# In a turn of the expert stage, work on finished sums is called ahead of the weight conversion

## The chip, the cores and the metric

The kernel runs on one core of a Trainium2 chip. The metric is the device time of one execution in microseconds (us), lower is better. TensorE does the matmuls, ScalarE and VectorE the elementwise work and the reading of PSUM, GpSimd (POOL) some small work, and SyncE (SP) starts the weight loads.

## The reference

It computes a decoder trunk of two layers on 256 tokens of width 1024 in float32. Only the last part matters here, the channel mixer of layer 1, a mixture of 8 experts of which each token takes 2:

```python
for e in range(N_EXPERTS):           # 8 experts, D_FF_EXPERT = 3584
    out = out + gates[:, e:e + 1] * _swiglu(t, w_gate[e], w_up[e], w_down[e])
# _swiglu(h, g, u, d) = (silu(h @ g) * (h @ u)) @ d
```

Ahead of it stand the mixers of both layers and a dense SwiGLU, and behind it a residual add and a final RMSNorm. The change touches none of these.

## The kernel before

**Precision.** A float32 product is made of fast float32r matmuls: each weight tile `raw` is split into a rounded part `wh` (ScalarE, line 190) and a remainder `wl` (VectorE, line 191). `Gran.conv` does this *conversion* of one tile, and also issues the tile's load on SP's queue if it isn't under way. Seven `raw` buffers hold loads, four `wh`/`wl` buffers hold converted tiles.

**Steps.** An expert's 3584 hidden columns are worked on in 4 chunks of 896. A *step* of TensorE uses one converted tile: four for the gate product (`g0` to `g3`, PSUM tile `pg`), four for the up product (`u0` to `u3`, `pu`), four for the down product of the expert before (`d0` to `d3`, `pd`, the last of half size). From expert 1 on a chunk runs in the order g0 g1 d0 g2 g3 d1 u0 u1 d2 u2 u3 d3. Expert 0 has eight steps a chunk, without the `d`; behind expert 7 stand its own down steps. An expert with at most 64 tokens is *few*: both halves of the split go through TensorE in one matmul, so a step has 8 matmuls in place of 12.

**Turns.** `emit` writes the order out by hand, one turn per step, and TensorE, ScalarE and VectorE keep the order in which they are called. Turn n called, before: the conversion of the tile of step n+3; the work in `mid[n]` (ScalarE and VectorE); the matmuls of step n; the folds; the TensorE work in `end[n]`. What stands in `mid` and `end`:

- `low`: ScalarE copies the lower half of a gate or up sum to `lo`, from which `fold_` adds it on TensorE (used for few).
- `post`: SiLU of the gate sum on ScalarE (line 1025), or the product with the up sum on VectorE (line 1027), both into `h`.
- `transposes`: `turn` turns `h` on TensorE into `pt` (line 971), `parts` splits that into `g2` for the down product, which runs four chunks later.
- `gather` for the next expert, in chunk 2: `select`, `rows_`, `parts`, `turn`, `copies`.
- `rows_of`: when the last down step of an expert has run, the two halves of its sum `yd` (both `pd` banks) are split into `h` by ScalarE (line 230) and VectorE (line 231). The next expert's first `d0` writes the same two banks and so waits for it.
- `scatter` (TensorE) and `residual_` (VectorE) put the result back on `x`.

`split` (lines 229 to 231) is the helper of `rows_of` and of both `parts`, and tells them apart only by the tile names.

Of the kernel before, what the change touches and what calls it, by code (L numbers as in the profile page):

```python
# [46 lines left out]
def trunk_kernel(ctx: ExitStack, tc, x_in, attn_norm, ffn_norm, w_in, b_in, conv_w, conv_b,  # L47
# [809 lines left out]
    def expert_steps(rnd):  # L857
# [8 lines left out]
        order, mid, end, folds, whose = [], {}, {}, {}, {}  # L866

        def at(where, n, f):
            where.setdefault(n, []).append(f)

        def put(e, run, gran):
            whose[len(order)] = e
            order.append((gran, run))

        def last():
            return len(order) - 1

        def emit():
            for n in range(max([len(order)] + [i + 1 for i in (*mid, *end, *folds)])):
                for g, _ in order[n:n + AHEAD_E + 1]:  # L880
                    g.conv()
                for f in mid.get(n, ()):
                    f()

                mine = [f for e, f in folds.get(n, ()) if whose.get(n) == e]
                if n < len(order):
                    g, run = order[n]
                    run(g.h, g.l, mine)
                for e, f in folds.get(n, ()):
                    if f not in mine:  # L890
                        by_count(e, lambda few, f=f: few and f())
                for f in end.get(n, ()):
                    f()
# [86 lines left out]
        def proj(e, c, nm, w, pool):  # L980

            wv = w[0, e, :, c * CH:(c + 1) * CH].rearrange("(k p) f -> p k f", p=P)
            st = {}

            def step(k2):
                def run(wh, wl, extra):
                    if k2 == 0:
                        st["p"] = [moe[pool].tile([P, 512], F32, name=pool) for _ in range(2)]

                    def mms(few):  # L990
                        for kk in range(2):
                            k = k2 * 2 + kk
                            x_ = xg[e][:, k]
                            both = x_.rearrange("p h s -> p (h s)")[:, 0:2 * P:2]
                            for hc in range(2):
                                o = slice(hc * HC, (hc + 1) * HC)
                                products(st["p"][hc][:, :HC], (x_[:, 0, :], x_[:, 1, :], both), wh[:, kk, o],
                                         wl[:, kk, o], k == 0, k == KD - 1, few)
                        for f in extra * few:
                            f()  # L1000
                    by_count(e, mms)
                put(e, run, Gran((rnd, e, c, nm, k2), (2, CH), lambda t: [(t, wv[:, k2 * 2:k2 * 2 + 2, :])],
                              lambda t: t, DVE))
                if k2 == KD // 2 - 1:
                    if rnd == 0:
                        at(mid, last() + 1, low)
                        at(folds, last() + 3, (e, fold_))
                    at(mid, last() + 4, post)

            def low():  # L1010
                for hc in range(2):
                    nc.scalar.activation(moe["lo"][HP:, hc * HC:(hc + 1) * HC], st["p"][hc][HP:, :HC], AF.Copy)  # L1012

            def fold_():
                for hc in range(2):
                    nc.tensor.matmul(st["p"][hc][:HP, :HC], fold, moe["lo"][:, hc * HC:(hc + 1) * HC],
                                     start=False, stop=True, skip_group_check=True)

            def post():
                if nm == "g":  # L1020
                    gg[e, c] = tmp.tile([P, CH], F32, name="h", bufs=3)
                for hc in range(2):
                    ps, o = st["p"][hc][:, :HC], slice(hc * HC, (hc + 1) * HC)
                    if nm == "g":
                        nc.scalar.activation(gg[e, c][:, o], ps, AF.Silu, scale=rxs[e])  # L1025
                    else:
                        nc.vector.scalar_tensor_tensor(gg[e, c][:, o], ps, rxs[e], gg[e, c][:, o],  # L1027
                                                       op0=ALU.mult, op1=ALU.mult)
            return [lambda k2=k2: step(k2) for k2 in range(KD // 2)]

        yd, ys, pys = {}, {}, {}

        def down(e, c):
            wv = moe_w_down[0, e, c * CH:(c + 1) * CH, :].rearrange("(j p) c -> p j c", p=P)
            both = (0, 1)
            parts = [(0, both), (2, both), (4, both), (6, both)]
            if (e, c) == (NE - 1, NCH - 1):

                parts[2:] = [(4, (0,)), (6, (0,)), (4, (1,)), (6, (1,))]

            def step(j0, chs):
                j1 = min(j0 + 2, KJ)

                def run(wh, wl, extra):
                    if c == 0 and j0 == 0:
                        for ch in chs:
                            yd[e, ch] = moe["pd"].tile([P, 512], F32, name="pd")

                    def mms(few):
                        for j in range(j0, j1):  # L1050
                            g_ = gt[e, c][:, j]
                            b = g_.rearrange("p s h -> p (s h)")[:, :P]
                            for i, ch in enumerate(chs):
                                o = slice(i * 512, (i + 1) * 512)
                                products(yd[e, ch], (g_[:, :, 0], g_[:, :, 1], b), wh[:, j - j0, o], wl[:, j - j0, o],
                                         c == 0 and j == 0, c == NCH - 1 and j == KJ - 1, few)
                        for f in extra * few:
                            f()
                    by_count(e, mms)
                put(e, run, Gran((rnd, e, c, "d", j0), (j1 - j0, D), lambda t: [(t, wv[:, j0:j1, :])],  # L1060
                              lambda t: t[:, :, chs[0] * 512:(chs[-1] + 1) * 512], DVE))
                if c == NCH - 1 and j1 == KJ:
                    n = last()
                    if e < NE - 1:
                        at(mid, n + 1, lambda: rows_of(e, both))
                        for ch in both:
                            at(end, n + 10 + 3 * ch, lambda ch=ch: scatter(e, ch))
                            at(mid, n + 11 + 3 * ch, lambda ch=ch: residual_(e, ch))
                    else:
                        at(mid, n + 1, lambda: rows_of(e, chs))  # L1070
                        at(end, n + 1, lambda: scatter(e, chs[0]))
                        at(mid, n + 2, lambda: residual_(e, chs[0]))
            return [lambda a=a: step(*a) for a in parts]
# [13 lines left out]
        def residual_(e, ch):  # L1087
            for t in range(NT):
                xs = x[:, t, ch * 512:(ch + 1) * 512]
                nc.vector.scalar_tensor_tensor(xs, pys[t], moe["gates"][:, t, e:e + 1], xs,  # L1090
                                               op0=ALU.mult, op1=ALU.add)
# [7 lines left out]
        for e in range(NE):  # L1099
            for c in range(NCH):  # L1100
                g = proj(e, c, "g", moe_w_gate, "pg")
                u = proj(e, c, "u", moe_w_up, "pu")
                d = down(e - 1, c) if e > 0 else []
                n0 = len(order)
                for fs, n in ((g, 2), (d, 1), (g, 2), (d, 1), (u, 2), (d, 1), (u, 2)):
                    do(fs, n)
                turn, parts = transposes(e, c)
                at(end, last() + 6, turn)
                at(mid, last() + 7, parts)
                do(d, 1)  # L1110
                if c == 2 and e + 1 < NE:
                    for (w, n), f in zip(((mid, 6), (end, 9), (mid, 10), (end, 12), (mid, 13)), gather(e + 1)):
                        at(w, n0 + n, f)
        for c in range(NCH):
            d = down(NE - 1, c)
# [2 lines left out]
        def run():  # L1118
            select, rows_, parts, turn, copies = gather(0)
            select()  # L1120
            for q in range(2):
                rows_((q,))
            parts()
            if rnd == 0:
                moe["flags"]()
                moe["weights"]()
            turn()
            copies()
            E = mybir.EngineType
            with tc.manual_schedule(engines={E.PE, E.Activation, E.DVE}):  # L1130
                emit()
# [58 lines left out]
```

## Time and profile before

| | |
|---|---|
| median of 3 runs | 1425.63 us (1423.59 to 1430.9) |
| the profiled execution's own time | 1431.23 us |
| its span, first to last instruction | 1429.5 us |
| its mean granted TensorE clock | 0.959 |

The profile shows one execution. Times in a timeline count from the start of the span. An engine's idle time is put down to the instruction that came last by the profile; where several are waited for, the name may be that of another.

### The profile page before, as it was taken

The page shows a single profiled execution, that of the slowest core. Times are in us where ns is not written, and L with a number is a line of the kernel's source. Part 1 is how long each engine was busy: PE and PEld are TensorE (multiplying, and loading weights), DVE is VectorE, ACT ScalarE, POOL GpSimd, SP SyncE. Part 2 cuts the span into 40 slices and gives each one's busy share as a digit, 9 for nine tenths or more (in the row PEclk, how much of TensorE's full clock was granted, in tenths as well). Part 3 has the DMA queues.
Part 4 walks back from the last instruction along what each step waited for, and adds up shares of the span by engine and source line. Part 5 has one row for each costly group of instructions (what it writes and reads, how often), then busy time and mean ns, then how long its engine had stood idle before and what let it go on. Part 6 is the DMA issues. An engine that isn't in the chain of part 4 may idle for free.

```text
span 1429.5 us, 18911 instructions
## 1 busy us (share of the span) xinstructions
PE 1315.3 (92%) x6899; PEld 1141.3 (80%) x6899; DVE 1164.2 (81%) x1155; ACT 1020.8 (71%) x1120; POOL 143.3 (10%) x98
## 2 busy tenths in 40 slices
PE   6989999989996879899999999899999899999986
PEld 6857999979765767687888889788888788888865
DVE  7785555567757878999999887899998999989975
ACT  5646444445745868898888777788887888878863
POOL 5551111117431000000000000000000000000000
PEclk9899999999898989999999999999999999999998
DMA  8823555663223998999999998899999999999991
GB/s 247 231 90 120 193 189 181 198 169 119 83 67 125 373 332 303 406 404 401 372 392 357 345 361 324 318 388 398 367 361 405 363 353 393 377 372 374 406 346 48
DMA packets 150176, 416.21 MB, mean 291 GB/s; under 512 B 8598, under 2 KB 49634, under 8 KB 150048
## 3 DMA queue, kind: packets, MB, share of 16 engines
q1 hardware_dynamic: 149760, 413.38, 79.6%
q8 instruction: 89, 1.46, 0.4%
q0 software_dynamic: 288, 1.05, 0.2%
q14 instruction: 39, 0.32, 0.1%
HBM read 413.35 MB, written 1.05 MB: 290 GB/s over the span
## 4 chain that ended last, share of the span: by engine, by line
PE 70%; DVE 11%; ACT 8%; issue 7%; DMA 2%; POOL 1%; SPq 0%; DVEq 0%; ACTq 0%; POOLq 0%
PE pu L909 17%; PE pd L909 16%; PE pg L909 9%; ACT wh L190 5%; DVE wl L191 5%; PE mm L693 4%; PE acc L718 4%; PE mm L351 4%; PE cv L693 4%; DVE cv L428 2%; PE pt L934 2%; PE acc L576 2%; PE pt L971 2%; PE acc L493 1%; DMA raw<-in_w_in_dram 1%
## 5 line engine op out<-in xcount | busy, mean ns | idle before, releaser
L191 DVE TENSOR_TENSOR wl<-raw,wh 128x1792 fp32r<-128x1792 f32 (+2 forms) x460 | 849.6, 1885 | 167.4 <-ACT wh L190 166.2
L190 ACT ACTIVATE wh<-raw 128x1792 fp32r<-128x1792 f32 (+2 forms) x496 | 755.9, 1555 | 302.5 <-PE pd L909 80.1
L909 PE MATMUL pd<-wh,g 128*128 128x512 f32 x672 | 246.2, 408 | 23.2 <-ACT wh L190 17.1
L909 PE MATMUL pu<-wh,xg 128*128 128x448 f32 x768 | 251.8, 374 | 9.9 <-DVE h L1027 9.9
L909 PE MATMUL pg<-wh,xg 128*128 128x448 f32 x768 | 250.6, 372 | 5.2 <-ACT h L1025 5.2
L909 PE MATMUL pu<-wl,xg 128*128 128x448 f32 x512 | 192.1, 375 | 2.8 <-DVE wl L191 2.8
L909 PE MATMUL pg<-wl,xg 128*128 128x448 f32 x512 | 191.1, 373 | 1.8 <-DVE wl L191 1.6
L909 PE MATMUL pd<-wl,g 128*128 128x512 f32 x448 | 181.4, 405 | 0.9 <-DVE wl L191 0.9
L909 PEld LDWEIGHTS pd<-wh,g 128*128 128x128 f32 x672 | 132.6, 197 | 51.9 <-ACT wh L190 19.3
L909 PEld LDWEIGHTS pu<-wh,xg 128*128 128x128 f32 x768 | 148.7, 194 | 24.4 <-ACT lo L1012 11.0
L909 PEld LDWEIGHTS pg<-wh,xg 128*128 128x128 f32 x768 | 148.3, 193 | 20.4 <-ACT h L1025 7.5
L909 PEld LDWEIGHTS pg<-wl,xg 128*128 128x128 f32 x512 | 99.5, 194 | 15.2 <-DVE wl L191 7.0
L909 PEld LDWEIGHTS pu<-wl,xg 128*128 128x128 f32 x512 | 100.8, 197 | 13.6 <-DVE wl L191 5.1
L909 PEld LDWEIGHTS pd<-wl,g 128*128 128x128 f32 x448 | 88.1, 197 | 18.3 <-DVE wl L191 2.9
L428 DVE SCALAR_TENSOR_TENSOR cv<-up,wcol,cv 128x256 f32<-128x256 f32 x226 | 98.3, 485 | 5.1 <-PE cv L402 3.1
L1147 POOL DMA_DIRECT2D h<-in_final_norm_dram x1 | 0.6, 599 | 964.2 <-PE pt L1085 964.2
L191 POOL TENSOR_TENSOR wl<-raw,wh 128x1024 fp32r<-128x1024 f32 x36 | 86.1, 2406 | 38.9 <-ACT wh L190 38.7
L351 PE MATMUL mm<-th,wh 128*128 128x256 f32 x224 | 65.9, 297 | 1.1 <-ACT sg L409 1.1
L351 PE MATMUL mm<-tl,wh 128*128 128x256 f32 x224 | 65.5, 293 | 0.8 <-DVE tl L288 0.8
L351 PE MATMUL mm<-th,wl 128*128 128x256 f32 x224 | 65.4, 293 | 0.9 <-POOL wl L191 0.7
L718 PE MATMUL acc<-wh,pp 128*128 128x512 f32 x176 | 50.3, 396 | 0.0
L693 PE MATMUL cv<-tl,wh 128*128 128x256 f32 x176 | 49.3, 280 | 0.3 <-DVE tl L288 0.3
(232 smaller groups left out, 1711.4 us busy)
## 6 DMA issues: line engine op xcount, KB each, us to landing
raw<-in_moe_w_gate_dram SPq DMA_DIRECT2D x128, 896.0 KB
raw<-in_moe_w_up_dram SPq DMA_DIRECT2D x128, 896.0 KB
raw<-in_moe_w_down_dram SPq DMA_DIRECT2D x96, 1024.0 KB
raw<-in_moe_w_down_dram SPq DMA_DIRECT2D x32, 512.0 KB
raw<-in_ffn_w_gate_dram SPq DMA_DIRECT2D x11, 1024.0 KB
raw<-in_ffn_w_up_dram SPq DMA_DIRECT2D x11, 1024.0 KB
raw<-in_ffn_w_down_dram SPq DMA_DIRECT2D x11, 1024.0 KB
raw<-in_w_in_dram SPq DMA_DIRECT2D x10, 1024.0 KB
```

What stands on the lines that cost most here:

```text
L190: nc.scalar.activation(self.h, src, AF.Copy)
L191: (lo or lo_eng()).tensor_sub(self.l, src, f32(self.h))
L351: nc.tensor.matmul(ps[:, :S], w(a, k), b[:, k, :], start=(n == 0), stop=(n == 3 * KD - 1))
L428: nc.vector.scalar_tensor_tensor(acc, up[:, c, k:k + S], w, acc, op0=ALU.mult, op1=ALU.add)
L493: nc.tensor.matmul(o, qT[hp, j, n * P:(n + 1) * P], kT[hp, k0:(n + 1) * P], start=False, stop=True)
L576: nc.tensor.matmul(st["o"][t][c], a[:, k, tk], b[:, 0, c * 512:(c + 1) * 512], start=(first and i == 0), stop=(last and i == 2))
L693: nc.tensor.matmul(ps, a[:, k, :], b[:, k, :], start=(n_ == 0), stop=(n_ == 3 * KD - 1))
L718: nc.tensor.matmul(st["o"][t][cc], a[:, kk, tk], b[:, 0, cc * 512:(cc + 1) * 512], start=(first and i == 0), stop=(last and i == 2))
L909: nc.tensor.matmul(ps, a, b, start=(first and i == 0), stop=(last and i == len(mm) - 1))
L934: nc.tensor.matmul(ps[:, j, :], moe["hn"][:, t, d], st["Sm"][:, t, :], start=(t == 0), stop=(t == NT - 1))
L971: nc.tensor.transpose(ps[:, j - j0, :], g[:, j * P:(j + 1) * P], ident)
L1147: nc.gpsimd.dma_start(fg, final_norm.unsqueeze(0).to_broadcast([P, D]))
```

## The change

In `emit` the `mid` work is called ahead of the conversion instead of behind it. Of the entries in `mid`, `low`, `post`, `residual_` and two of `gather` are put one turn later. `parts` of the transposes goes two turns later and `turn`, its TensorE half in `end`, one. `rows_of`, `select`, and the `residual_` behind the very last steps keep their turn.

```diff
             for n in range(max([len(order)] + [i + 1 for i in (*mid, *end, *folds)])):
+                for f in mid.get(n, ()):
+                    f()
                 for g, _ in order[n:n + AHEAD_E + 1]:
                     g.conv()
-                for f in mid.get(n, ()):
-                    f()
...
-                        at(mid, last() + 1, low)
+                        at(mid, last() + 2, low)
                         at(folds, last() + 3, (e, fold_))
-                    at(mid, last() + 4, post)
+                    at(mid, last() + 5, post)
...
                         at(mid, n + 1, lambda: rows_of(e, both))
                         for ch in both:
                             at(end, n + 10 + 3 * ch, lambda ch=ch: scatter(e, ch))
-                            at(mid, n + 11 + 3 * ch, lambda ch=ch: residual_(e, ch))
+                            at(mid, n + 12 + 3 * ch, lambda ch=ch: residual_(e, ch))
...
-                at(end, last() + 6, turn)
-                at(mid, last() + 7, parts)
+                at(end, last() + 7, turn)
+                at(mid, last() + 9, parts)
                 do(d, 1)
                 if c == 2 and e + 1 < NE:
-                    for (w, n), f in zip(((mid, 6), (end, 9), (mid, 10), (end, 12), (mid, 13)), gather(e + 1)):
+                    for (w, n), f in zip(((mid, 6), (end, 9), (mid, 11), (end, 12), (mid, 14)), gather(e + 1)):
```

## Rows read from the trace of the kernel before

**Rows 1.** The page: engines' busy time, and the chain that ended last.
```profile
PE 1315.3 (92%) x6899; PEld 1141.3 (80%) x6899; DVE 1164.2 (81%) x1155; ACT 1020.8 (71%) x1120; POOL 143.3 (10%) x98
...
PE 70%; DVE 11%; ACT 8%; issue 7%; DMA 2%; POOL 1%; SPq 0%; DVEq 0%; ACTq 0%; POOLq 0%
```

**Rows 2.** Two stretches: length, busy us by engine, PEclk, DMA share, GB/s.
```profile
550.00:975.00 425.00, 403.29 (x1940) 349.91 (x1939) 387.07 (x264) 352.76 (x307) 0.00 (x0) 0.99 0.98 369
975.00:1365.00 390.00, 374.97 (x1817) 328.71 (x1815) 360.75 (x248) 326.06 (x285) 0.00 (x0) 0.99 1.00 379
```

**Rows 3.** Waits, 550 to 1365: us in total, times, longest.
```profile
DVE wl L191 <- ACT wh L190: 66.3, 68, 4.4
ACT wh L190 <- PE pd L909: 60.7, 42, 3.3
...
PE pd L909 <- ACT wh L190: 17.1, 6, 4.2
...
PE pt L971 <- DVE h L1027: 13.5, 13, 1.8
```

**Rows 4.** Groups by form, 550 to 1365: busy us, mean ns, idle before.
```profile
L191 DVE TENSOR_TENSOR wl<-raw,wh 128x1792 fp32r<-128x1792 f32 x220 | 437.1, 2021 | 31.2 <-ACT wh L190 30.5
...
L1027 DVE SCALAR_TENSOR_TENSOR h<-pu,rx,h 128x448 f32<-128x448 f32 x56 | 35.6, 678 | 0.0
L191 DVE TENSOR_TENSOR wl<-raw,wh 128x1024 fp32r<-128x1024 f32 x28 | 34.2, 1222 | 0.0
...
L231 DVE TENSOR_TENSOR h<-pd,h 128x512 fp32r<-128x512 f32 x12 | 7.7, 683 | 0.0
```

**Rows 5.** ScalarE's timeline, end of an expert: start, length, idle before.
```profile
897.17 1.92 ACT L190 ACTIVATE wh<-raw 128x2048 fp32r<-128x2048 f32 x1 [2.15 <-PE pd L909]
899.12 0.97 ACT L1012 ACTIVATE lo<-pu 64x448 fp32r<-64x448 f32 x2
900.12 1.70 ACT L190 ACTIVATE wh<-raw 128x1792 fp32r<-128x1792 f32 x1
901.84 1.09 ACT L230 ACTIVATE h<-pd 128x512 fp32r<-128x512 f32 x2
```

**Rows 6.** VectorE's timeline at the same place.
```profile
899.13 2.29 DVE L191 TENSOR_TENSOR wl<-raw,wh 128x2048 fp32r<-128x2048 f32 x1 [2.04 <-ACT wh L190]
901.85 2.03 DVE L191 TENSOR_TENSOR wl<-raw,wh 128x1792 fp32r<-128x1792 f32 x1 [0.43 <-ACT wh L190]
903.79 1.28 DVE L231 TENSOR_TENSOR h<-pd,h 128x512 fp32r<-128x512 f32 x2
...
913.39 3.96 DVE L191 TENSOR_TENSOR wl<-raw,wh 128x1792 fp32r<-128x1792 f32 x2 [2.99 <-ACT wh L190]
```

**Rows 7.** TensorE's timelines: the first matmul into `pd` of each expert's sum.
```profile
656.49 0.47 PE L909 MATMUL pd<-wh,g 128*128 128x512 f32 x1 [1.67 <-ACT wh L190]
...
774.24 0.48 PE L909 MATMUL pd<-wh,g 128*128 128x512 f32 x1 [2.57 <-ACT wh L190]
...
904.62 0.77 PE L909 MATMUL pd<-wh,g 128*128 128x512 f32 x1 [4.25 <-ACT wh L190]
...
1021.31 0.47 PE L909 MATMUL pd<-wh,g 128*128 128x512 f32 x1 [2.16 <-ACT wh L190]
...
1140.99 0.48 PE L909 MATMUL pd<-wh,g 128*128 128x512 f32 x1 [4.24 <-ACT wh L190]
...
1256.93 0.47 PE L909 MATMUL pd<-wh,g 128*128 128x512 f32 x1 [2.17 <-ACT wh L190]
...
1371.02 0.76 PE L909 MATMUL pd<-wh,g 128*128 128x512 f32 x1 [6.15 <-DVE h L231]
```

**Rows 8.** TensorE's timeline: transposes in an expert with few tokens.
```profile
941.70 1.25 PE L971 MATMUL pt<-ident,h 128*128 128x128 f32 x7 [1.79 <-DVE h L1027]
```

**Rows 9.** Short stretches at two of those stalls, columns as in rows 2.
```profile
900.00:910.00 10.00, 5.75 (x15) 4.36 (x15) 9.57 (x8) 6.27 (x6) 0.00 (x0) 0.66 0.96 344
910.00:925.00 15.00, 15.00 (x75) 13.57 (x75) 12.01 (x9) 13.27 (x13) 0.00 (x0) 1.00 0.76 258
1015.00:1030.00 15.00, 12.84 (x56) 10.83 (x55) 11.80 (x10) 10.42 (x10) 0.00 (x0) 0.89 1.03 408
```

## The prediction

> **What bounds the kernel now.** I read the page first, then the waits, then timelines at the places that the waits name. The page has TensorE busy for 92% and on 70% of the chain that ended last, VectorE on 11% [rows 1]. That is a mean over stages; the change lies in the expert stage alone, so the stage comes next, cut at 550 and 1365 us (experts 1 to 7). There TensorE is busy for 403.29 + 374.97 = 778 of 815 us, VectorE for 387.07 + 360.75 = 748, ScalarE for 679, GpSimd for nothing, and the DMA share is 0.98 to 1.00 [rows 2]. Three resources lie within 8% of each other: what one of them gains is worth something only where the other two have room.
>
> TensorE's missing 37 us are what is to be had. The waits name two places [rows 3]: 17.1 us in 6 waits ahead of a matmul into `pd`, and 13.5 us in 13 waits of the transposes for `post`. The third large wait, ScalarE's conversion for TensorE (60.7 us), is that of an engine held back by a full set of `wh` buffers, and only follows TensorE.
>
> The timelines show the 6 waits, and a seventh at 1371.02, as one pattern: 1.67, 2.57, 4.25, 2.16, 4.24, 2.17 and 6.15 us, once per expert, always before the first down step `d0` of a new sum [rows 7]. Six are put down to ScalarE's conversion, the seventh to VectorE's `h`. I take the seventh to be right for all. At 904.62 the conversion of `d0`'s own tile (the one of 2048) had ended on ScalarE at 897.17 + 1.92 = 899.09, and on VectorE at 899.13 + 2.29 = 901.42, 3.2 us earlier [rows 5, 6]. What ended last is `rows_of`: VectorE began it at 903.79, and at 0.683 us a half [rows 4] its first bank was free at 904.47.
>
> **The change part by part.** First, what does not move. A turn was "conversion n+3, then mid n" and becomes "mid n, then conversion n+3". An entry that goes from mid n to mid n+1 at the same time is called between the conversions n+3 and n+4 in both versions. This holds for `low`, `post`, `residual_` and the gather's `parts` and `copies`: ScalarE and VectorE get the same instructions in the same order, in both kernels. No sum is read later than it was, and nothing waits less. The entries behind the last steps have no conversion left to pass. All of it: 0 us. SP's queue holds the loads alone, in the order of the conversions, so that isn't touched; GpSimd has no work in the stage [rows 2].
>
> What moves on its engine is what was not shifted by exactly one.
>
> (a) `rows_of` keeps turn n+1 and so passes one conversion, that of `g2` behind `d0`. Before, ScalarE's order was: conversion `d0` (897.17), `low` (899.12), conversion `g2` (900.12), `rows_of` (901.84) [rows 5], and VectorE's `d0`, `g2` (901.85), `rows_of` (903.79) [rows 6]. After: ScalarE is through with `low` at 900.09 and does its two copies by 901.2; VectorE ends `d0` at 901.42 and frees the first bank at 901.42 + 0.68 = 902.10, the second at 902.8. 904.47 becomes 902.10: 2.4 us earlier. It adds no wait, since the conversion of `d0` ahead of it has already waited for the same down step (2.15 us behind `pd`, at 897.17 [rows 5]). Behind it the conversion of `g2` comes 1.1 us later on ScalarE and about 1.3 us on VectorE, and TensorE wants it next.
>
> At the first six places the stall shrinks by up to 2.4 us: 1.67 + 2.4 + 2.4 + 2.16 + 2.4 + 2.17 = 13.2. At the seventh the tile passed is a half one, 1.222 us on VectorE [rows 4]: 1.2. Together 14.4. Then what is late next: `g2`. VectorE ends the two halves at 902.8 and `g2`'s remainder 2.02 us later, 904.8, which is 902.10 + 2.7. A down step of 12 matmuls takes longer than that, and one of 8 about 2 us, so at the three places where the finished down product is that of an expert with few tokens (656.49, 1021.31, 1256.93) some 0.4 us comes back: 13.2 in all, to the nearest.
>
> The clock is a second term. At the stall of 1021.31 the granted clock is 0.89 over 15 us, so 0.11 x 15 = 1.65 us of full-speed time goes with it; around 904.62 it is 0.66 over 10 us [rows 9], part of that while TensorE is idle anyway. Of the two levels, 1.2 and 2.4 GHz, it fell to the lower behind the idle time. The stalls at 1021.31 and 1256.93 should vanish, and with them 2 x 1.65 = 3.3 us. Those at 904.62 and 1140.99 keep 1.8 us and the last keeps 5, so I count nothing there. Bounds for the clock: 0, if the remaining gaps trip it as before, and 5 x 1.65 = 8.3. I take 3.3, because the two stalls that disappear are the ones that the row prices.
>
> Is there room on VectorE and in the loads for 13.2 + 3.3 = 16.5 us? Behind the stall of 904.62 VectorE stood for 2.99 us (913.39) and before it for 0.43 [rows 6], since ScalarE ran out of free buffers behind the stalled TensorE: there the stall is passed on whole, and about 3 us is what that place can give. And the DMA share fell to 0.76, 258 GB/s, in 910 to 925, for the same reason [rows 9]. So both have idle time at just these places, and it goes with the stall.
>
> (b) `turn`, the seven transposes, goes one TensorE step later, and `parts` one conversion later; `g2` is needed four chunks on, so nothing waits for it. Before, TensorE stood up to 1.79 us for `post` [rows 8], 13.5 us in 13 waits [rows 3]. After, it runs `d1` first, whose conversion stands ahead of `post` on VectorE and so is done, and `post` (two at 0.678 us [rows 4]) ends meanwhile. But these waits lie in experts with few tokens, where a TensorE step is shorter than a conversion's 2.02 us on VectorE [rows 4]: what TensorE saves it mostly waits later for `wl`. Bounds: 0 and 13.5. I take 2, nearer to 0, since VectorE is busy for 748 of 815 us [rows 2].
>
> (c) `select`, three VectorE instructions on 128 columns each, passes one conversion, as `parts` of (b) moves the other way by one. Each is shorter than the 0.678 us of `post` on 448 columns: under 2 us in 7 places, in a stretch in which the tile then late has the room that `parts` left. 0, bounds -1 and +2.
>
> Sum: 13.2 + 3.3 + 2 = 18.5 us. From the profiled execution's own 1431.23 that makes 1412.7; that execution lies 5.6 us above the median of the runs, so on runs like those it is 1425.63 - 18.5 = 1407, and I say 1408.
>
> **The rivals.** *The loads bind.* The DMA share is near 1 already [rows 2]; if the queue cannot go faster, what TensorE saves at a stall is waited for at a later load. For it: share 0.98 to 1.00. Against: the mean is (425 x 369 + 390 x 379) / 815 = 374 GB/s, while 408 is reached in a short stretch [rows 9], so at 408 the stage's bytes take 815 x 374 / 408 = 747 us, 68 us less. Room on average, though not in every chunk. If a third of the 18.5 arrives: 1420. The Trainium skill's page "DMA: Bandwidth & Descriptors" (section "Where 436 GB/s comes from") would have it bind: for transfers from HBM it gives about 358 GB/s for a core. By that rule this stage would be at its limit now and the change worth nothing, 1426. The rows, with 369 and 379 over hundreds of us and 408 in a stretch, are above the rule, for a core that runs alone; I go by them.
>
> *The change does nothing.* Most of its lines leave the order as it was, as shown; if the order of `rows_of` does not set the stall either, it is 1425.6. Against it: the seventh row names `rows_of`.
>
> *Slower: the profile's name is right, and `d0` does wait on ScalarE's conversion.* Six of seven rows say so [rows 7]. Then `rows_of`, put ahead of the conversion of `g2`, delays it by its own 1.28 us on VectorE [rows 6], seven times: 9 us, 1435. It decides if the stalls before `d0` stay as long as they were with `rows_of` done early. Against it: the tile's conversion was over 3.2 us before.
>
> *More than that.* The clock gives its whole 8.3 and the transposes half of their 13.5: 13.2 + 8.3 + 6.8 = 28, 1397.
>
> **How the numbers follow.** The forecast, 1402 to 1414, gets 0.68; more than that 0.10; the loads 0.10; nothing 0.06; slower 0.06. The range goes from 1398 to 1420: it takes in the forecast, nearly all of the larger gain and the case of the loads, and leaves out some 0.15. A change under 0.5%, about 7 us, is what a measurement of this kernel can't tell from none. Faster by more: the forecast, the larger gain, and a few hundredths of the loads, 0.82. Within 0.5%: the loads' rest and nothing, 0.12. Slower: 0.06.
>
> **What would show it.** In the profile of the changed kernel, ScalarE's `h<-pd` should stand right behind `lo<-pu` and ahead of the 1792-wide conversion; the idle time before the first `pd` matmul should be 0 at about four places, some 1.8 at two and 5 at the last; the granted clock should stay at 1.00 around the places that were 1021 and 1257. The wait of `pt` for `h L1027` should be gone, and small waits of `pu` or `pd` for `wl` should have grown. The order of all else on ScalarE and VectorE should be as before. The prediction is wrong if `d0` stalls as long as ever, if waits for `raw` appear on ScalarE, or if a conversion that found its buffer free before now waits for TensorE a step longer.

## The result, and the profile after

The changed kernel takes 1393.28 us, the median of 6 runs (1385.47 to 1395.55), against 1423.32 us for the kernel before beside it (6 runs, 1418.65 to 1430.9). The ratio is 0.977, with a 95% interval of 0.9741 to 0.98: about 33 us, or 28 to 37, where 18.5 were predicted. The direction was right; the time lies below the range. The profiled execution took 1386.59 us.

The page of the changed kernel, beside [rows 1]:

```profile
PE 1295.2 (94%) x6899; PEld 1124.6 (81%) x6899; DVE 1162.6 (84%) x1155; ACT 1019.3 (74%) x1120; POOL 143.3 (10%) x98
```

The work is the same (the counts of instructions are those of before), but TensorE is busy for 20 us less. Two profiled executions differ also in front of the expert stage, where the code is the same, so from here on the stage is cut from the first matmul into `pg` to the last scatter matmul. The windows of the whole stage, first of the kernel before and then of the changed one (columns: stretch, length, busy us of PE, PEld, DVE, ACT and POOL, granted clock, DMA share, GB/s):

```profile
453.34:1417.88 964.54, 905.74 (x4325) 787.91 (x4323) 861.18 (x593) 783.30 (x689) 0.60 (x1) 0.98 0.95 357
```

```profile
440.74:1373.40 932.66, 897.26 (x4325) 779.81 (x4323) 859.17 (x593) 782.00 (x689) 0.60 (x1) 0.99 0.96 369
```

The stage is 31.9 us shorter. TensorE's busy time fell by 8.5 us and its idle time by 23.4. The stretches that answer to [rows 2], and the one that answers to the second of [rows 9]:

```profile
530.00:955.00 425.00, 413.20 (x2000) 357.05 (x2001) 398.09 (x275) 364.71 (x319) 0.00 (x0) 1.00 1.00 378
955.00:1345.00 390.00, 382.33 (x1866) 335.24 (x1865) 371.91 (x253) 335.66 (x292) 0.00 (x0) 0.99 1.01 394
1000.00:1015.00 15.00, 15.00 (x76) 13.31 (x75) 15.00 (x11) 12.47 (x12) 0.00 (x0) 1.00 1.03 407
```

In as many us TensorE does more instructions than before, and behind the place that was 1021 (now 999.62) the granted clock stays at 1.00, where it was 0.89. The waits in 530 to 1345, beside [rows 3] (us in total, times, longest):

```profile
DVE wl L191 <- ACT wh L190: 44.2, 50, 5.7
ACT wh L190 <- PE pd L909: 38.0, 31, 5.3
...
PE pu L909 <- DVE wl L191: 4.6, 10, 1.1
PE pd L909 <- ACT wh L190: 4.1, 1, 4.1
PE pd L909 <- DVE wl L191: 3.6, 9, 1.0
```

The wait of the transposes (L971) for `h` is gone. Of the waits before the first matmul into `pd` one long one is left, the last. The wait that the prediction set aside, ScalarE's conversion for the down matmuls, fell as well, from 60.7 us [rows 3] to 38.0. The timelines of ScalarE and of VectorE at the place of [rows 5, 6], and TensorE's at five of the seven places of [rows 7]:

```profile
877.51 1.93 ACT L190 ACTIVATE wh<-raw 128x2048 fp32r<-128x2048 f32 x1 [0.76 <-PE pu L909]
879.46 0.98 ACT L1012 ACTIVATE lo<-pu 64x448 fp32r<-64x448 f32 x2
880.46 1.09 ACT L230 ACTIVATE h<-pd 128x512 fp32r<-128x512 f32 x2
881.43 3.31 ACT L190 ACTIVATE wh<-raw 128x1792 fp32r<-128x1792 f32 x2
```

```profile
879.47 2.29 DVE L191 TENSOR_TENSOR wl<-raw,wh 128x2048 fp32r<-128x2048 f32 x1 [0.66 <-ACT wh L190]
881.68 1.28 DVE L231 TENSOR_TENSOR h<-pd,h 128x512 fp32r<-128x512 f32 x2
883.17 6.16 DVE L191 TENSOR_TENSOR wl<-raw,wh 128x1792 fp32r<-128x1792 f32 x3 [0.21 <-ACT wh L190]
```

```profile
641.32 0.39 PE L909 MATMUL pd<-wh,g 128*128 128x512 f32 x1
...
756.03 0.48 PE L909 MATMUL pd<-wh,g 128*128 128x512 f32 x1 [0.70 <-PEq L899]
...
882.78 0.48 PE L909 MATMUL pd<-wh,g 128*128 128x512 f32 x1 [0.67 <-DVE h L231]
...
1106.39 0.48 PE L909 MATMUL pd<-wh,g 128*128 128x512 f32 x1 [0.86 <-DVE h L231]
...
1325.67 0.76 PE L909 MATMUL pd<-wh,g 128*128 128x512 f32 x1 [4.10 <-ACT wh L190]
```

`rows_of` stands where the prediction put it, and the stalls are 0.70, 0.67, 0.86 and 4.10 us and none at the three others. But look at the first line of ScalarE. In [rows 5] the conversion of `d0` began after 2.15 us of waiting, for a matmul into `pd`; here it waited 0.76 us, for one into `pu`. Nothing in the diff touches that conversion. It wants a free buffer, and it now wants another one.

The addresses in the two built programs say which. Most of the stage's 386 conversions write the buffers of the conversion four turns back, as a ring of four would. In the kernel before 34 take those of the conversion *three* turns back: 27 conversions of `d0` (every chunk from expert 1 on but the first), 6 of a `u0`, and one of expert 7's own down steps. The one behind each of them takes those of five turns back. I call the 34 *early*: an early one cannot start before TensorE is a step further on. The changed kernel has 8 such places.

### The profile page after: what moved, and what is told of

It is laid out like the page before. It is cut to its first block, busy times and chain, and to the rows that moved or that the text cites. A ratio compares the mean times of both kernels' runs of the same rounds, so it can differ in the third digit from the quotient of the medians.

```text
span 1384.9 us, 18931 instructions
## 1 busy us (share of the span) xinstructions
PE 1295.2 (94%) x6899; PEld 1124.6 (81%) x6899; DVE 1162.6 (84%) x1155; ACT 1019.3 (74%) x1120; POOL 143.3 (10%) x98
## 5 line engine op out<-in xcount | busy, mean ns | idle before, releaser
L909 PE MATMUL pd<-wh,g 128*128 128x512 f32 x672 | 239.3, 397 | 6.3 <-ACT wh L190 4.1
```

The lines of the kernel that those rows point to most:

```text
L909: nc.tensor.matmul(ps, a, b, start=(first and i == 0), stop=(last and i == len(mm) - 1))
```

## The experiments

Theory 1: the 31.9 us are the sum of `rows_of`, the transposes, and the choice of buffers. Theory 2, the rival: order alone made the gain, and the buffers are a by-product that costs nothing. All timed against the kernel before; "us" is (1 - ratio) x 1423; by the intervals one such number is good to 3 to 6 us, and a difference of two to some 5 to 9. The last two columns are from one profiled execution each, which is not always near the median: that of e3 took 1406.63 us, 9 above its median, most of it ahead of the stage, which began at 452.80 us there and at 444.23 in e1.

| kernel | early places | median us | ratio (95%) | us | stage us | TensorE busy |
|---|---|---|---|---|---|---|
| before | 34 | 1423 | 1 | | 964.5 | 905.7 |
| control, named buffers (e9) | 34 | 1426.18 | 1.0024 (0.9996 to 1.0052) | -3.4 | 965.7 | 906.5 |
| + `rows_of` (e11) | 34 | 1411.33 | 0.9928 (0.9899 to 0.9957) | 10.2 | 949.5 | 902.2 |
| + transposes (e12) | 34 | 1413.20 | 0.9942 (0.9918 to 0.9966) | 8.3 | 953.5 | 902.6 |
| changed order (e10) | 34 | 1400.02 | 0.9846 (0.9812 to 0.988) | 21.9 | 939.3 | 899.5 |
| before's order, in turn (e1) | 0 | 1401.18 | 0.9849 (0.9806 to 0.9892) | 21.5 | 939.9 | 893.7 |
| + `rows_of` (e2) | 0 | 1391.99 | 0.9772 (0.9735 to 0.9809) | 32.4 | 932.7 | 894.2 |
| + transposes (e3) | 0 | 1397.54 | 0.9807 (0.9772 to 0.9843) | 27.5 | 940.5 | 898.7 |
| changed order, in turn (e4) | 0 | 1387.48 | 0.9732 (0.9687 to 0.9777) | 38.1 | 929.0 | 895.2 |
| `rows_of`, pool's choice (e7) | 28 | 1411.16 | 0.9924 (0.9902 to 0.9946) | 10.8 | 950.3 | 901.5 |
| transposes, pool's choice (e8) | 14 | 1401.12 | 0.9845 (0.982 to 0.9871) | 22.1 | 943.6 | 899.8 |
| the changed kernel | 8 | 1393.28 | 0.977 (0.9741 to 0.98) | 32.7 | 932.7 | 897.3 |

**Buffers in turn (e1).** `Ring` hands out eight named tiles, four `wh` and four `wl`, in strict turn. Every engine has the same instructions in the same order as in the kernel before.

```diff
-        hl[0] = ctx.enter_context(tc.tile_pool(name="hle", bufs=AHEAD_E + 1, reuse_waits="tile"))
+        hl[0] = Ring(ctx.enter_context(tc.tile_pool(name="hle", bufs=1, reuse_waits="tile")), AHEAD_E + 1)
...
+    def tile(self, sh, dt, name):
+        free = self.free[name]
+        i = free.pop(1 if self.k[name] in self.early else 0)
+        self.k[name] += 1
+        free.append(i)
...
```

> The kernel before, with its order of work untouched: the four pairs of buffers for converted weights are taken strictly in turn in the expert stage, where before takes, at 34 of 386 conversions, the buffer freed last (that of the conversion three turns back instead of four). Theory 1 (the missed part of the gain is the choice of buffers): 34 conversions wait one step less, 26 of them not early any more in the changed kernel; by the shift of 0.3 to 0.5 us a place seen in the chunks without rows_of, 8 to 14 us faster than before, about 1412 us, and ScalarE's wait for the down product falls from 60.7 us to under 35. Theory 2 (the rows_of and the transposes make the whole gain, buffers are a by-product): within 3 us of before, about 1423.

Measured: 21.5 us (15 to 28) with no instruction moved, more than I expected.

**`rows_of` alone, and the transposes alone, over buffers in turn (e2, e3), and the changed order over them (e4).** In e2 a list `pre` is called ahead of the conversion and holds `rows_of` alone; e3 shifts two turns. e4 is the changed kernel with `Ring`.

```diff
+                for f in pre.get(n, ()): f()
                 for g, _ in order[n:n + AHEAD_E + 1]:
...
-                        at(mid, n + 1, lambda: rows_of(e, both))
+                        at(pre, n + 1, lambda: rows_of(e, both))
```

```diff
-                at(end, last() + 6, turn)
-                at(mid, last() + 7, parts)
+                at(end, last() + 7, turn)
+                at(mid, last() + 8, parts)
```

> The same kernel with buffers in turn, and in addition rows_of alone taken past one conversion (it stands ahead of it); transposes and parts stay. Theory 1: 12 to 16 us below the run with buffers in turn alone, about 1398; the wait of the first down product of each expert, 1.7 to 6.2 us in the kernel before, falls under 1 us. Theory 2: 18 to 25 us below that run. A third theory, that the transposes hold the most: at most 5 us below it.

> The kernel before with buffers in turn, and in addition the transposes alone one step later and the copies behind them one conversion later; rows_of stays where it was. Theory 1: 2 to 5 us below the run with buffers in turn alone, about 1408. Theory 2: 5 to 10 us below it. Third theory (the transposes hold the most): 15 us or more below it.

> The changed kernel with buffers in turn: only its 8 remaining early places go. Theory 1: 0 to 4 us below the changed kernel, about 1391, and equal within 3 us to before less the gains of the three runs beside it added up. Theory 2: as the changed kernel, 1393.

Measured against e1, by the ratios: `rows_of` 11.0 us, the transposes 6.0, and both with the rest of the change 16.6. So they add up, and 38.1 is 21.5 + 11.0 + 6.0 to within a us. In the profiled stages `rows_of` is worth 7.2 us and the transposes nothing (-0.6); that the transposes bring anything over buffers in turn is not shown, since the intervals of e1 and e3 overlap by much. (Those of e1 and e2 just touch, but every run of e2 is below every run of e1.) e4 is the fastest kernel here. It lies 5.4 us below the changed kernel by the ratios and 3.7 in the stage, but the intervals overlap.

**The early choice written out (e5, e6).** The named buffers, taken early at the 34 places, with the conversion still called ahead of the matmuls that read the buffer it takes.

```diff
+        hl[0] = Ring(ctx.enter_context(tc.tile_pool(name="hle", bufs=1, reuse_waits="tile")), AHEAD_E + 1, EARLY)
```

> A control for the four runs with buffers in turn: the kernel before with the same eight named buffers, but taken as before takes them, the one freed last at the same 34 places. Theory 1 (it is the choice that counts): as before, 1423 within 4 us. Theory 2 (naming the buffers changes something else, the waits that the builder places for instance, and that made the 21.5 us): about 1401, as the run with buffers in turn.

> The changed kernel, its order of work untouched, with the named buffers taken at the 34 places of the kernel before. Theory 1: only rows_of (9.2 us by the run before) and the transposes (3.6 us) remain of the gain, so about 13 us faster than before, 1410; the buffers are worth about 17 us to the changed kernel. Theory 2: as the changed kernel, 1393.

Measured: 1576.80 us (ratio 1.1068, 1.103 to 1.1106) and 1572.73 us (1.1046, 1.1023 to 1.1069), foreseen by neither theory. Called in that order, 34 steps multiply by the tile of the conversion three turns on, and TensorE waits for it: in e5 it waits for `wl` 28 times ahead of `pd` and 6 times ahead of `pg`, 89.2 us together. These are other kernels than the ones I meant, and they say nothing on what the choice of buffers is worth. They suggest that the pool of the kernel before did not plan these conversions ahead of the matmuls, as they are called.

**The control mended (e9), and the changed kernel with before's buffers (e10).** At the 34 places the conversion is called behind the matmuls of the step whose buffer it takes (the lines are e9's, where the `mid` work of these turns moves with it). Each engine again has the order of before, or of the changed kernel.

```diff
+                early = n + AHEAD_E in EARLY
+                for g, _ in order[n:n + AHEAD_E + 1 - early]: g.conv()
...
                     run(g.h, g.l, mine)
+                for g, _ in order[n + AHEAD_E:][:early]: g.conv()
```

> The control mended: named buffers, taken as in before at 34 places, and at these places the conversion is called behind the matmuls that still read its buffer, so that it overwrites nothing too soon; each engine has the same instructions in the same order as in before. Theory 1 (the choice of buffers counts): as before, 1423 within 4 us. Theory 2 (the naming of the buffers made the 21.5 us): about 1401.

> The changed kernel with its order of work untouched on every engine, but with the named buffers taken at the 34 places of the kernel before, called in the same mended way. Theory 1: rows_of (9.2 us in the run with buffers in turn) and the transposes (3.6) alone remain of the gain: about 13 us faster than before, 1410. Theory 2: as the changed kernel, 1393.

Measured: e9 is as before within its interval, and its trace repeats the waits of before. So what e1 gained comes from the choice of buffers and not from naming them. e10 keeps 21.9 us (17 to 27), between the two expectations. So the choice of buffers is worth 10.8 us to the changed kernel, 6.7 in the profiled stages (939.3 to 932.7), and the order alone 21.9, or 26.3 in the stages. Theory 2 falls, and so does my 13 for the order: over early buffers it is worth more than over buffers in turn (26.3 us in the stages against 11.0, e1 to e4).

**The two halves of the order over before's buffers (e11, e12).** The edits of e2 and e3 on the control e9.

> The mended control (named buffers taken early at the 34 places, as in before), and rows_of alone past one conversion. The order of the changed kernel was worth 23 us over these buffers and 13.7 us over buffers in turn. Theory 1, rows_of carries it, as the prediction had it (16.5 of 18.5): 14 to 18 us below before, 1407. Theory 2, the two halves share it because early conversions make the wait of the transposes longer: about 10 us below, 1413.

> The mended control, and the transposes alone one step later, their copies one conversion later. Theory 1 (rows_of carries it): 2 to 5 us below before, 1419, as over buffers in turn (3.6). Theory 2 (shared): about 10 us or more below, 1412, and the two runs together add up to the 23 us.

Measured: 10.2 us (6 to 14) and 8.3 us (5 to 12); against the control e9, 13.7 and 11.7, which add up to e10's 25.3. In the profiled stages 16.1 and 12.2, against 26.3 for both. The halves share the gain. TensorE's waits over the stage, the control e9 first, then e11, then e12:

```profile
PE pd L909 <- ACT wh L190: 17.1, 6, 4.2
PE pt L971 <- DVE h L1027: 13.6, 13, 1.8
...
PE pd L909 <- DVE h L231: 6.2, 1, 6.2
...
PE pu L909 <- DVE wl L191: 3.0, 3, 1.1
PE pg L909 <- DVE wl L191: 1.6, 5, 0.6
PE pd L909 <- DVE wl L191: 0.9, 2, 0.5
```

```profile
PE pt L971 <- DVE h L1027: 14.6, 14, 2.2
...
PE pd L909 <- ACT wh L190: 5.0, 1, 5.0
PE pd L909 <- DVE h L231: 4.2, 3, 1.8
PE pu L909 <- DVE wl L191: 3.7, 4, 1.1
PE pg L909 <- DVE wl L191: 1.8, 6, 0.4
PE pd L909 <- DVE wl L191: 0.9, 2, 0.5
```

```profile
PE pd L909 <- ACT wh L190: 17.0, 6, 4.2
...
PE pd L909 <- DVE h L231: 6.2, 1, 6.2
PE pu L909 <- DVE wl L191: 4.1, 9, 1.1
PE pd L909 <- DVE wl L191: 4.0, 10, 0.9
PE pg L909 <- DVE wl L191: 1.6, 4, 0.8
```

Each edit takes away its own wait (`rows_of` all but 9.2 us of it) and leaves the other's.

**Each half under the pool's own choice (e7, e8).** The edits of e2 and e3 made to the kernel before, without `Ring`.

> The kernel before, with the pool's own choice of buffers, and rows_of alone taken past one conversion. With it the pool makes 28 early choices in place of 34. Theory 1: 9.2 us for rows_of and 6 of 34 of 21.5 us, 3.8, for the buffers: 13 us below before, 1410. If all of the gain had come with rows_of: 1393.

> The kernel before, with the pool's own choice of buffers, and the transposes alone one step later, the copies behind them one conversion later. With it the pool makes 14 early choices in place of 34. Theory 1: 3.6 us for the transposes and 20 of 34 of 21.5 us, 12.6, for the buffers: 16 us below before, 1407. If the buffers counted for nothing: 1419.

Measured: 10.8 us (8 to 14), and 22.1 us (18 to 26) for the transposes, above my 16. Read beside e12: the same edit is worth 8.3 us when it may not change the buffers and 22.1 when it may. The transposes alone lose 20 early places (34 to 14) and `rows_of` alone the 6 of the `u0` (34 to 28); together these are the 26 that the change loses. The places are not worth the same: the 6 show no gain of their own (e7 10.8 us, e11 10.2).

**What an early buffer costs.** ScalarE's and VectorE's groups of the 2048-wide conversions (`d0` to `d2`) over the stage, in the control e9 and then in e1 (count, busy us, mean ns, idle before and what ended it):

```profile
L190 ACT ACTIVATE wh<-raw 128x2048 fp32r<-128x2048 f32 x95 | 182.3, 1919 | 80.4 <-PE pd L909 66.1 <-PE pg L909 8.1 <-DMA raw<-in_moe_w_down_dram 3.5
...
L191 DVE TENSOR_TENSOR wl<-raw,wh 128x2048 fp32r<-128x2048 f32 x95 | 217.2, 2287 | 46.7 <-ACT wh L190 46.7
```

```profile
L190 ACT ACTIVATE wh<-raw 128x2048 fp32r<-128x2048 f32 x95 | 182.6, 1922 | 59.5 <-PE pu L909 25.1 <-PE pg L909 15.5 <-PE pd L909 12.8
...
L191 DVE TENSOR_TENSOR wl<-raw,wh 128x2048 fp32r<-128x2048 f32 x95 | 217.6, 2290 | 27.6 <-ACT wh L190 27.2
```

The instructions are the same and as long. ScalarE's wait for the step into `pd` falls from 66.1 to 12.8 us; part of it becomes a wait for the steps ahead, and 21 us are gone. VectorE's idle time behind it falls by 19. VectorE's waits for ScalarE's conversion over the whole stage, and ScalarE's own for TensorE:

```profile
DVE wl L191 <- ACT wh L190: 95.0, 91, 7.0
ACT wh L190 <- PE pd L909: 86.6, 62, 6.5
...
ACT wh L190 <- PE pu L909: 25.0, 26, 4.1
```

```profile
DVE wl L191 <- ACT wh L190: 69.0, 91, 6.4
ACT wh L190 <- PE pu L909: 52.4, 47, 4.3
ACT wh L190 <- PE pd L909: 40.5, 35, 5.9
```

in e9 and in e1: VectorE waits 26.0 us less, and the stage is 25.7 us shorter. The same holds for the change as a whole:

```profile
DVE wl L191 <- ACT wh L190: 95.5, 91, 5.9
```

```profile
DVE wl L191 <- ACT wh L190: 65.7, 68, 5.7
```

in the kernel before and in the changed one, 29.8 us of the 31.9. VectorE's busy time and this wait, 861.2 + 95.5, make 957 of the 964.5 us before and 859.2 + 65.7 = 925 of the 932.7 after. VectorE does the same work in all these kernels, so a shorter stage has to show in its idle time; that the change of buffers is the cause rests on e1, e9 and e10. What the rows add is where the time was: nearly all of VectorE's idle time is this one wait.

## Why the prediction fell short, point by point

**(a) `rows_of`: right in mechanism and, in the stage, in size.** e11 is this edit alone, over before's buffers. The stalls before `d0` were to shrink by 14.4 us; they went from 17.1 + 6.2 to 5.0 + 4.2, by 14.1. They were to be 0 at about four places, some 1.8 at two and 5 at the last. The trace of e11, at three of them:

```profile
887.11 0.48 PE L909 MATMUL pd<-wh,g 128*128 128x512 f32 x1 [1.79 <-DVE h L231]
...
1117.26 0.48 PE L909 MATMUL pd<-wh,g 128*128 128x512 f32 x1 [1.79 <-DVE h L231]
1232.52 0.39 PE L909 MATMUL pd<-wh,g 128*128 128x512 f32 x1
```

The first, fourth and sixth are 0, the second is 0.66, and the last 5.0. So the reading of [rows 7], that `rows_of` and not the named conversion ended last, holds. What was to come back as waits for `wl`, 1.2 us, was 0.9 (3.0 + 1.6 + 0.9 became 3.7 + 1.8 + 0.9). The clock was to give 3.3; TensorE's busy time fell by 4.3 us. Against that the wait of the transposes grew by 1.0. The stage is 16.1 us shorter for the 16.5 predicted. By the timed runs it is 10.2 us against the kernel before (6 to 14, short of 16.5) and 13.7 against the control, with an interval that takes in 16.5. One reason given was an accident of the early buffer: that `rows_of` adds no wait because `d0`'s conversion has waited for the same down step. In the changed kernel that conversion waits for `pu`; `rows_of` still adds no wait, since ScalarE's `h` waits for `pd` 3.9 us in 2 waits in both kernels.

**(b) The transposes: right in the mechanism, wrong in size.** "I take 2" failed: e12 measures 8.3 us (11.7 against the control, 12.2 in the stage), inside the bounds of 0 and 13.5. The wait of 13.6 us went, as foretold. The step "what TensorE saves it mostly waits later for `wl`" did not hold: those waits rose from 5.5 to 9.7 us, so 4.2 of 13.6 came back, and the busy time gave another 3.9. I had read VectorE's 748 of 815 us as nearly full. But it spent 66.3 of the other 67 us waiting for ScalarE [rows 3], 95.0 us over the whole stage in e9, and ScalarE in turn waited for buffers that TensorE still held. In e12 this wait of VectorE's is 82.9 us, 12.1 less, with the transposes the only thing moved: the idle time went with TensorE's wait.

**"All of it: 0 us": the step that failed, by 7 to 11 us.** For the entries that it names (`low`, `post` and the others shifted by exactly one) the 0 holds: the 26 early places that go are the 6 of `rows_of` and the 20 of the transposes, and e10's gain over the control is 25.3 us where the two halves add up to 25.3 (26.3 and 28.3 in the stages). But the conversions keep their order too, and what keeps its place in each engine's order was held to cost the same. Their buffers are not the same, at 26 places, and the sum has no term for that. The difference from e10 to the changed kernel is 10.8 us by the ratios (the intervals of the two just fail to meet at 0.98 and 0.9812), 6.7 in the stages. The last line of the prediction named a conversion that waits a step longer as what would make it wrong. It was the reverse: conversions of the kernel *before* waited a step longer than a ring of four asks. The signs of it were in the rows: the 2.15 us behind `pd` ahead of `d0`'s conversion [rows 5], where the step four turns back was one into `pu`; and 60.7 us in 42 waits [rows 3], which the prediction put aside as "an engine held back by a full set of `wh` buffers, and only follows TensorE". e1 shows that this wait was in part a cause: over the stage it is 86.6 us in e9 and 40.5 in e1, of which 27.4 come back as waits for `pu`, and the stage is 25.7 us shorter with the order untouched.

**Sum.** 16.5 + 2 became 16.1 + 12.2 in the stages (26.3 together), and the buffers added 6.7, where e10's 26.3 and 6.7 make 33.0 and the difference from before 31.9. The predicted mechanisms are about four fifths of the gain by the stages, and two thirds by the timed runs (21.9 of 32.7). e10, with the order alone, took 1400.02 us, inside the stated range; it is the buffers that take the time out of it.

**The rivals.** *The loads bind* did not come about: the second half of the stage ran at 394 GB/s for 390 us, above the 379 of before [rows 2], and ScalarE's waits for `raw` in the changed kernel are small (8.8 us in 14 waits over the stage, 4.4 in 8 before). In e4, the fastest, they are longer:

```profile
ACT wh L190 <- DMA raw<-in_moe_w_down_dram: 15.3, 24, 1.0
ACT wh L190 <- DMA raw<-in_moe_w_up_dram: 8.0, 17, 0.7
```

The loads may be what comes next; no run here tests it. The Trainium skill's page "DMA: Bandwidth & Descriptors" (section "Where 436 GB/s comes from") has about 358 GB/s, the bandwidth of a stack divided by two cores, bind a core's transfers from HBM. The measurement decides against it here: 369 GB/s over the whole stage of the changed kernel and 394 over 390 us, on a core that runs alone. *Slower, because the named conversion ends last* is refuted by e11. *More than that* is nearest, but not for its reasons: the transposes gave about what it assumed or more, TensorE's busy time fell by 8.5 us, with all edits together, where it assumed 8.3 for the clock, and the buffers, which it did not have, gave the rest.

**Open.** Why the pool takes the later of two buffers at these places was not tested. At 28 of the 34 the buffers taken are those of a half-size `d3`. It looks as if, in the order in which the builder plans the instructions, two buffers are free there and the one freed last is handed out. That is argued from the addresses. `select`, costed at 0, was not run by itself; what e10 has beyond the two halves is 0.0 us by the ratios and -2.0 in the stages.

## What to carry to other kernels

Where an engine waits for a free buffer, look at which step it waits for and count: with four buffers it should be the step four back. If it is a later one, the pool's choice costs a step of run-ahead at each such place, and any edit nearby can change the choice, for better or worse; compare the addresses of the two builds, or fix the ring by hand, before an edit's gain is put down to its order. And before an edit is priced low because another engine "is nearly full", read what that engine's idle time waits for: if it waits for the very thing that the edit frees, both are had, as in e12.

## What the runs showed that I had not expected

Taking four buffers in strict turn, with no instruction moved, is worth 21.5 us of 1423 (15 to 28), as much as all the reordering over before's buffers (21.9). The two overlap: together they make 38.1, not 43. And TensorE's busy time, for the same matmuls, moved between 906.5 us in e9 and 893.7 in e1, with a mean granted clock over the stage of 0.98 of full speed and of 0.99. It does not simply follow the idle time: e4 has less of that than e1 (33.8 us against 46.3) and a busy time of 895.2. The stages of e9 and of e1:

```profile
446.98:1412.66 965.68, 906.50 (x4324) 786.95 (x4322) 861.07 (x593) 782.88 (x689) 0.60 (x1) 0.98 0.95 356
```

```profile
444.23:1384.17 939.94, 893.65 (x4325) 782.37 (x4323) 861.31 (x593) 785.73 (x689) 0.60 (x1) 0.99 0.96 366
```
